# A planner's build-time estimate of the matrix products' pace, replaced by longer steps

## The chip, the core and the metric

The kernel runs on one core of a Trainium2 chip. The metric is the device time of one execution in microseconds (us), lower is better; times of several runs are given as their median.

## The reference

A decoder trunk of two layers in float32, for 256 tokens of 1,024 features, with a memory of 256 rows. Cut to its outline:

```python
for l in range(2):
    h = rms_norm(x, norm_mix[l])
    if l == 0:
        b, c, u = split(h @ conv_w_in, 3)
        x = x + (b * conv3(c * u)) @ conv_w_out
    else:
        x = x + causal_attention(rope(h @ moba_w_q), k, v) @ moba_w_o
    x = x + softmax(q(rms_norm(x)) @ mem_k.T / 16) @ mem_v @ mem_w_o[l]
    g, u = split(rms_norm(x, norm_ffn[l]) @ ffn_w_gu[l], 2)
    x = x + (silu(g) * u) @ ffn_w_down[l]
    if l == 0:
        k, v = split(rms_norm(x, kv_norm) @ w_kv, 2)
        k = rope(k)
return rms_norm(x, norm_final)
```

The feed-forward part has 2,816 hidden features, the memory attention 4 heads of 256, the causal attention 8 heads of 128.

## The kernel before

**Products.** Every large product is made from operands in two float32r parts, a high one and the rest, in three passes: high by low, low by high, high by high. There are two forms. `mm3` (L321) multiplies 128 tokens by up to 512 output features, three products of that width; by `mm_rows` (L419) it serves the projections and `down` (the feed-forward's second half), and with 256 columns the first gate and up products. `mm_cols` (L425) puts output features on partitions: one product of 512 columns (high weights by both parts of 256 tokens) and one of 256 (low weights by the high part), eight such pairs for 128 features; it serves the convolution's gates (tiles `cu`, `pb`), the memory queries (`q_acc`) and most of the gate and up products (`gu`). The keys of the memory (`mem_keys`, L638) use single products of 256 columns. All of them are issued by `mm` (L313, its instruction is L314), transposes by `transpose` (L317, L318).

**Stages.** In order: keys of layer 0's memory (`acc_memk`), the convolution, its output projection (`acc_cout`), the memory's values (`acc_memv`), memory attention, feed-forward (`gu`, `ff`); then layer 1's keys, queries and values (`acc_k`, `acc_q`, `acc_v`), beside the values and the next memory keys the causal attention, its output (`acc_o`), the memory's values, memory attention, feed-forward and the last norm.

**Weights.** They come in chunks of 1,024 columns, 512 KB each, loaded by SyncE (L331) into five raw buffers. ScalarE casts a chunk to its high part, VectorE subtracts to get the low part, and the next raw load follows a low part. Ten chunks may be split ahead of the products (`Feed`, L173).

**Side work.** All that is not this stream (norms, transposes of activations, rotary turns, softmax, the small products of attention) is written as generators. `Side.poll` (L138) is called after each product and lets every generator go on whose time has come; `Feed.pump` then splits a weight chunk if ScalarE or VectorE is free by the estimate and no side step is due within 300 ns. So the place of each instruction in its engine's queue is settled when the program is built, by an estimated clock (`Clock`, L45). The clock keeps for each engine the time at which it is free, and for each written tile the time at which it can be read: an instruction starts when its engine is free and its inputs are ready, and its output is ready 140 ns after its end, 200 ns for TensorE. "Now" is the time at which TensorE is free. `Timed` (L82) estimates ScalarE at 50 + 0.875 ns a column, VectorE at 67 + 1.04, GpSimd at 460, each with 80 more for an operand of one column. A side step that yields nothing goes on at the first poll at which now has reached the readiness of its last instruction; some yield a fixed number of nanoseconds. Where the main stream needs what a side job has not written yet, `Act.need` (L244) lets the job run to its end at once, and TensorE then waits on the chip.

TensorE's costs are given where a product is issued. For a product of n columns:

```python
ns = 0.4167 * math.prod(b[0].shape[1:]) + 2     # mm3
0.4167 * 2 * T + 2,  0.4167 * T + 2             # mm_cols, T = 256
0.4167 * T + 2                                  # mem_keys
```

that is 215.4 ns for 512 columns and 108.7 for 256. Transposes are noted at 109 ns, the causal attention's small products at 218 (436 with 256 columns), and all is doubled while now is under 4,700 ns.

**Side groups named below.** `turned` (L1184): ScalarE copies a bank of keys or queries out of the accumulator (`r`), VectorE turns 32 columns of each head in four steps, TensorE transposes (`pt_r`). `Normed.run` (L761): squares, mean, GpSimd's power (`rs`), the normed rows `hn` on VectorE, transposes (`pt_h`). `attend` in `mem_attention` (L975) and in `moba` (L1213): scores `s`, softmax, transposes of the probabilities (`pt_p`, `pt`), their copy or split `pT`, the product with the values (`po`). `start_rstd` (L615): two diagonals in one buffer, each multiplied by ones (`pb_rs`). `tables` (L791): small loads and, when they should have landed, two small transposes (`pt_c`).

Of the kernel before, what the change touches and what calls it, by code (L numbers as in the profile page):

```python
# [21 lines left out]
KD = D // P  # L22
T = 256
# [10 lines left out]
RAWS = 5  # L34
# [10 lines left out]
class Clock:  # L45
    """Estimates of where the engines stand, in nanoseconds, to choose the order of instructions by."""

# [34 lines left out]
class Timed:  # L82
    """An engine whose instructions are noted on the clock."""

# [23 lines left out]
class Side:  # L108
    """Work beside the main stream of matrix products, as generators. A bare yield waits for the last
    instruction, a number for that many nanoseconds."""  # L110

# [44 lines left out]
    def hold(self, kind):  # L156
        """wait for a free buffer; each is listed with the time from which it is free"""
        free = self.free[kind]
        while not free or min(free) > self.clock.now:
            yield 0 if not free else min(free) - self.clock.now  # L160
        free.remove(min(free))
# [11 lines left out]
class Feed:  # L173
    """The weights in the order of their use: loaded RAWS chunks ahead of their split into two parts,
    which goes on while the engines have nothing else, as far ahead of the products as there are buffers."""

# [58 lines left out]
class Act:  # L235
    """An activation, transposed and in two float32r parts; jobs[half, bank] still fill it."""

# [17 lines left out]
def yoco_kernel(  # L255
# [26 lines left out]

# [1 line left out]
    def acc_tile(name):  # L284
# [26 lines left out]

# [1 line left out]
    def mm(o, l, r, start, stop, ns):  # L313
# [7 lines left out]
    def mm3(o, a, b, start, stop):  # L321
        """a.T @ b of operands in two parts each"""
        ns = 0.4167 * math.prod(b[0].shape[1:]) + 2
        mm(o, a[0], b[1], start, False, ns)
        side.poll()
        mm(o, a[1], b[0], False, False, ns)
        side.poll()
        mm(o, a[0], b[0], False, stop, ns)
# [5 lines left out]

    # ---- weights: a chunk of 1024 columns a partition; a norm's weight goes in here where the
    # chunk's rows are its features ----
    def row_plan(name, w, c0, gain=None, pieces=1, halves=1):
# [42 lines left out]
    def ffn_steps():  # L380
        """pairs of 128 columns: gate and up ahead of down by a pair or more; the last downs come bank by bank"""
        steps, n = [], 0
        for jp in range(NP):
            steps.append(("gu", jp))
            while jp >= ROW_PAIRS and n < min(jp - 2, NP - LAG):
                steps.append(("down", n))
                n += 1
        return steps, list(range(n, NP))
# [28 lines left out]

# [1 line left out]
    def mm_rows(acc, act, k, h, w, b, start, stop):  # L419
        """acc[token, 512 features] += act[token, k-th 128] @ w[k-th 128, 512 features]"""  # L420
        act.need(k, (h,))
        mm3(acc, act.parts(k, tok(h)), [r[:, 0, bank(b)] for r in w], start, stop)
        side.poll()

    def mm_cols(acc, act, w, j):  # L425
        """acc[128 features, (both parts, token)]: its halves' sum is w[:, 128 features].T @ act.T, of the
        chunk's j-th 128"""
        for k in range(KD):
            act.need(k)
            x_both = act.units[k // 4][:, k % 4].rearrange("p r t -> p (r t)")  # L430
            hi, lo = (r[:, k % 4, j * P:(j + 1) * P] for r in w[k // 4])
            mm(acc.rearrange("p r t -> p (r t)"), hi, x_both, k == 0, False, 0.4167 * 2 * T + 2)
            side.poll()
            mm(acc[:, 0, :], lo, act.parts(k)[0], False, k == KD - 1, 0.4167 * T + 2)
            side.poll()
# [15 lines left out]
    def proj_rows(act, name, done, order=STRAIGHT):  # L451
        """act @ w by token halves, k tiles and banks in the order given; done(half, bank, accumulator)"""
        chunks, accs = {}, {}
        for h, k, b in order:
            if (h, b) not in accs:
                accs[h, b] = acc_tile(f"acc_{name}_{h}_{b}")
            if k not in chunks:
                chunks[k] = feed.take(f"{name}_{k}")
            if h == 1 and b == 1:
                feed.free()  # L460
            mm_rows(accs[h, b], act, k, h, chunks[k], b, k == 0, k == KD - 1)
            if k == KD - 1:
                done(h, b, accs[h, b])

    def turn_parts(src, dst, h, g, gain=None):
        """src [128 tokens, 512] to both parts of bank g of dst, features on partitions"""
        yield from side.hold("tp")
        pt = tp_tile("pt_h")
        for i in range(4):
            transpose(pt[:, i, :], src[:, i * P:(i + 1) * P])  # L470
        yield
        if gain is not None:
            yield from side.hold("half")
            t = held_half("xg", (P, 4, P))
            g0 = gain_col(gain, 4 * g)
            g4 = bass.AP(tensor=g0.tensor, offset=g0.offset, ap=[g0.ap[0], [1, 4], [0, P]])
            vector.tensor_mul(t, pt, g4)
            side.give("tp")
            yield
            pt = t  # L480
        yield from split_steps(dst.units[g][:, :, 0, tok(h)], dst.units[g][:, :, 1, tok(h)], pt,
                               "tp" if gain is None else "half")
# [7 lines left out]

# [1 line left out]
    def square_half(src, ss, b):  # L492
# [20 lines left out]

    # ---- constants; the memory, transposed as it is: its norm's weight is in the products' weights and
    # its rows' factors come after the products ----
    ident = const.tile([P, P], F32, name="ident")
# [47 lines left out]
    def warm_up(n):  # L564
        """products that no one reads, for the tensor engine's clock"""
        for _ in range(n):
            transpose(warm[:, :P], ident)
# [68 lines left out]

# [1 line left out]
    def mem_keys(name, mT, wait, ready=None):  # L638
# [16 lines left out]
        def step(k, w, j, passes=((0, 0), (0, 1), (1, 0))):  # L655
            """a bank's two column tiles are one accumulation group: its start clears both"""
            acc = accs[j // 2][:, (j % 2) * T:(j % 2 + 1) * T]
            mT.need(k)
            x = mT.parts(k)
            for a, b in passes:  # L660
                mm(acc, w[a][:, 0, j * P:(j + 1) * P], x[b], k == a == b == 0 and j % 2 == 0,
                   k == KD - 1 and a == 1 and j % 2 == 1, 0.4167 * T + 2)
                side.poll()
# [39 lines left out]

# [1 line left out]
    x_sb = const.tile([P, 2, D], F32, name="x_sb")  # L705
# [12 lines left out]
    class Plain:  # L718
        """x itself, transposed, times a norm's weight if it is not in the products' weights; its rows'
        factors come after the products"""  # L720

# [15 lines left out]
    class Normed:  # L737
        """the normed rows, transposed"""

# [45 lines left out]

# [1 line left out]
    cs = const.tile([P, 2, 2, ROT], F32, name="cs")  # L787
# [82 lines left out]

# [1 line left out]
    def short_conv(act, into):  # L872
# [56 lines left out]

# [1 line left out]
    def softmax(s, p, scale, minus):  # L931
        """scale, minus: the scores' factor and its negative, numbers or a column for each of s's two parts"""
        mx = small.tile([P, 2], F32, tag="mx", name="mx")
# [19 lines left out]

# [1 line left out]
    def mem_attention(l, kT, values, src, into):  # L955
# [77 lines left out]

# [1 line left out]
    def swiglu(l, src, done, fine_end=False, at_end=None):  # L1035
# [21 lines left out]
        def gate_up_rows(jp, w, h):  # L1057
            """one token half, tokens on partitions: it can run before the other half is normed"""
            side.grab("gu")
# [114 lines left out]

# [1 line left out]
    def moba(src, into):  # L1176
# [7 lines left out]
        def turned(dst, key):  # L1184
            """the rows' four heads of a bank, their first 32 columns turned, transposed"""
            def turn(h, b, acc, r):
# [109 lines left out]

# [1 line left out]
    fin = {}  # L1298
# [61 lines left out]
```

## Time and profile before

| | |
|---|---|
| median of three runs | 803.84 us (803.82 to 804.37) |
| span of the profiled execution, first to last instruction | 802.4 us |
| TensorE busy | 792.4 us, 99% |
| VectorE busy | 537.7 us, 67% |
| ScalarE busy | 444.7 us, 55% |
| DMA engines | 54% of 16 engines' span, 143.4 MB |
| granted TensorE clock, mean | 0.996 of 2.4 GHz |

The profiled execution has no time of its own beside its span; the runs' median is 1.4 us longer than that span. PE is TensorE's products, PEld its weight loads (they overlap the products), DVE VectorE, ACT ScalarE, POOL GpSimd, SP SyncE. Matmuls are pipelined and their ends are modelled, so a product is shown for some 390 ns where the next starts after some 227: the pace is read from the starts, or from stretches of many products.

### The profile page before, as it was taken

Reading aid. Unit: us, or ns where it says so; the run is one execution under the profiler, and the core shown is the slowest. Engines: PE = TensorE matmul, PEld = TensorE weight load, DVE = VectorE, ACT = ScalarE, POOL = GpSimd, SP = SyncE. Lnnn points to the kernel's source line nnn. Section 1 sums busy time; section 2 is a strip of 40 time slices with the busy share of each in tenths; the row PEclk is TensorE's granted clock in tenths of the full one; section 3 lists DMA queues with packets and bytes.
Section 4 is the critical chain, followed back from the end, with each engine's and each line's share of the span. In section 5 each row is a group of like instructions: output and inputs, shape, how many; then the busy total and the mean of one; then the engine's idle time right before and its main releaser. Section 6 shows DMA issues by size and latency. Waiting matters only on the chain.

```text
span 802.4 us, 11670 instructions
## 1 busy us (share of the span) xinstructions
PE 792.4 (99%) x4497; PEld 690.8 (86%) x4497; DVE 537.7 (67%) x833; ACT 444.7 (55%) x730; POOL 17.6 (2%) x42
## 2 busy tenths in 40 slices
PE   8999999999999999999999999999999999999996
PEld 7988888898998888888888889888989988888885
DVE  4897987776758655666566667777757576556633
ACT  5766555664656545555554566556645565455432
POOL 0100001000100000000000000010000000000000
PEclk9999999999999999999999999999999999999999
DMA  8666666734547665555466316567344476655611
GB/s 304 222 207 213 214 206 207 244 102 135 155 136 253 197 213 171 160 194 202 136 202 202 139 53 218 176 210 257 112 124 151 138 243 207 210 162 167 199 55 52
DMA packets 90219, 143.40 MB, mean 179 GB/s; under 512 B 4844, under 2 KB 70452, under 8 KB 90164
## 3 DMA queue, kind: packets, MB, share of 16 engines
q1 hardware_dynamic: 89876, 142.14, 54.3%
q8 instruction: 35, 0.57, 0.3%
q10 hardware_dynamic: 288, 0.52, 0.2%
q14 instruction: 20, 0.16, 0.1%
HBM read 141.60 MB, written 1.05 MB: 178 GB/s over the span
## 4 chain that ended last, share of the span: by engine, by line
PE 98%; DMA 1%; SPq 0%; DVE 0%; issue 0%; POOLq 0%; ACT 0%; DVEq 0%; ACTq 0%
PE gu L314 31%; PE ff L314 15%; PE q_acc L314 6%; PE cu L314 6%; PE acc_mo L314 6%; PE acc_memv L314 5%; PE acc_memk L314 5%; PE pb L314 3%; PE acc_v L314 3%; PE acc_q L314 3%; PE acc_cout L314 3%; PE acc_k L314 3%; PE acc_o L314 3%; PE po L314 2%; PE s L314 2%; PE pt_h L318 2%
## 5 line engine op out<-in xcount | busy, mean ns | idle before, releaser
L314 PE MATMUL ff<-hi_wd,guT 128*128 128x512 f32 (+1 forms) x352 | 108.1, 387 | 0.0
L314 PE MATMUL gu<-ffn,hi_wu 128*128 128x512 f32 x288 | 103.2, 398 | 0.0
L314 PE MATMUL gu<-ffn,hi_wg 128*128 128x512 f32 x288 | 103.1, 397 | 0.0
L314 PE MATMUL gu<-ffn,lo_wg 128*128 128x256 f32 x288 | 81.0, 281 | 0.0
L314 PE MATMUL gu<-ffn,lo_wu 128*128 128x256 f32 x288 | 80.8, 281 | 0.0
L314 PEld LDWEIGHTS ff<-hi_wd,guT 128*128 128x128 f32 x352 | 65.7, 188 | 13.4
L103 DVE TENSOR_TENSOR gu_sb<-gu_sb,gu 128x256 f32<-128x256 f32 x72 | 30.3, 421 | 69.6 <-ACT gu_sb L103 69.1
L103 ACT CAST hi_wu<-raw_wu 128x1024 fp32r<-128x1024 f32 x52 | 53.4, 1050 | 35.5 <-PE ff L314 25.0
L103 DVE TENSOR_TENSOR lo_wu<-raw_wu,hi_wu 128x1024 fp32r<-128x1024 f32 x52 | 61.5, 1221 | 14.6 <-ACT hi_wu L103 14.6
L314 PE MATMUL ff<-lo_wd,guT 128*128 128x512 f32 (+1 forms) x176 | 68.4, 388 | 0.0
L103 ACT COPY gu_sb<-gu 128x256 f32<-128x256 f32 x72 | 26.8, 373 | 71.7 <-PE gu L314 71.7
L314 PEld LDWEIGHTS gu<-ffn,hi_wu 128*128 128x128 f32 x288 | 54.1, 188 | 13.4
L314 PEld LDWEIGHTS gu<-ffn,hi_wg 128*128 128x128 f32 x288 | 54.1, 188 | 12.9
L103 DVE TENSOR_TENSOR lo_wd<-raw_wd,hi_wd 128x1024 fp32r<-128x1024 f32 x44 | 53.4, 1221 | 10.1 <-ACT hi_wd L103 10.1
L314 PEld LDWEIGHTS gu<-ffn,lo_wg 128*128 128x128 f32 x288 | 54.4, 189 | 0.5
L314 PEld LDWEIGHTS gu<-ffn,lo_wu 128*128 128x128 f32 x288 | 54.4, 189 | 0.0
L103 DVE TENSOR_TENSOR lo_wg<-raw_wg,hi_wg 128x1024 fp32r<-128x1024 f32 x44 | 52.6, 1219 | 1.1 <-ACT hi_wg L103 1.1
L314 PE MATMUL acc_memk<-mT,hi_memk 128*128 128x256 f32 x256 | 47.8, 291 | 1.8 <-ACT hi_memk L103 1.8
L103 ACT CAST hi_wd<-raw_wd 128x1024 fp32r<-128x1024 f32 x44 | 45.8, 1046 | 4.2 <-PE ff L314 4.2
L103 ACT CAST hi_wg<-raw_wg 128x1024 fp32r<-128x1024 f32 x44 | 45.6, 1051 | 0.6 <-PE acc_mo L314 0.6
L314 PE MATMUL q_acc<-mem,hi_mq 128*128 128x512 f32 x128 | 45.9, 399 | 0.0
L314 PEld LDWEIGHTS acc_memk<-mT,hi_memk 128*128 128x128 f32 x256 | 40.0, 195 | 2.1 <-ACT hi_memk L103 2.0
(229 smaller groups left out, 1823.7 us busy)
## 6 DMA issues: line engine op xcount, KB each, us to landing
raw_wg<-in_ffn_w_gu_dram SPq DMA_DIRECT2D x44, 512.0 KB, 4.8
raw_wu<-in_ffn_w_gu_dram SPq DMA_DIRECT2D x44, 512.0 KB, 3.7
raw_wd<-in_ffn_w_down_dram SPq DMA_DIRECT2D x44, 512.0 KB, 4.3
raw_memv<-in_mem_w_kv_dram SPq DMA_DIRECT2D x16, 512.0 KB, 4.6
raw_mq<-in_mem_w_q_dram SPq DMA_DIRECT2D x16, 512.0 KB, 5.0
raw_mo<-in_mem_w_o_dram SPq DMA_DIRECT2D x16, 512.0 KB, 4.7
raw_memk<-in_mem_w_kv_dram SPq DMA_DIRECT2D x14, 512.0 KB, 5.4
raw_wc<-in_conv_w_in_dram SPq DMA_DIRECT2D x8, 512.0 KB, 3.7
```

Of the source, the lines that this page charges most:

```text
L103: return call(out, *args, **kw)
L314: nc.tensor.matmul(o, l, r, start=start, stop=stop)
L318: nc.tensor.transpose(o, i, ident[:i.shape[0], :i.shape[0]])
```

## The change

A function gives the cost of a product of n columns on the estimated clock, and the three forms use it. No instruction is added or removed by the diff itself. What else the diff holds are comments and texts of functions that are dropped. The core:

```diff
+    def mm_ns(n):
+        return n / 2.4 + 13.5
...
     def mm3(o, a, b, start, stop):
-        ns = 0.4167 * math.prod(b[0].shape[1:]) + 2
+        ns = mm_ns(math.prod(b[0].shape[1:]))
...
     def mm_cols(acc, act, w, j):
...
-            mm(acc.rearrange("p r t -> p (r t)"), hi, x_both, k == 0, False, 0.4167 * 2 * T + 2)
+            mm(acc.rearrange("p r t -> p (r t)"), hi, x_both, k == 0, False, mm_ns(2 * T) + 8)
             side.poll()
-            mm(acc[:, 0, :], lo, act.parts(k)[0], False, k == KD - 1, 0.4167 * T + 2)
+            mm(acc[:, 0, :], lo, act.parts(k)[0], False, k == KD - 1, mm_ns(T) - 3)
             side.poll()
...
         def step(k, w, j, passes=((0, 0), (0, 1), (1, 0))):
...
                 mm(acc, w[a][:, 0, j * P:(j + 1) * P], x[b], k == a == b == 0 and j % 2 == 0,
-                   k == KD - 1 and a == 1 and j % 2 == 1, 0.4167 * T + 2)
+                   k == KD - 1 and a == 1 and j % 2 == 1, mm_ns(T))
                 side.poll()
```

The estimates become 226.8 ns for 512 columns and 120.2 for 256, and 234.8 and 117.2 for the pair in `mm_cols`.

## Rows read from the trace of the kernel before

**Rows 1.** The page, parts 1 and 4: busy engines; the chain's shares.

```profile
PE 792.4 (99%) x4497; PEld 690.8 (86%) x4497; DVE 537.7 (67%) x833; ACT 444.7 (55%) x730; POOL 17.6 (2%) x42
...
PE 98%; DMA 1%; SPq 0%; DVE 0%; issue 0%; POOLq 0%; ACT 0%; DVEq 0%; ACTq 0%
```

**Rows 2.** TensorE's waits: us in total, times, longest us.

```profile
PE acc_memk L314 <- ACT hi_memk L103: 1.8, 1, 1.8
```

**Rows 3.** The chain in order of time: start us, us, what, how many.

```profile
46.27 5.55 PE cu L314 x32
...
104.51 11.38 PE acc_cout L314 x50
...
261.33 11.29 PE gu L314 x64
...
488.07 16.67 PE acc_memk L314 x139
```

**Rows 4.** Timeline, a turned pair of layer 1's keys: start us, us, what [idle before].

```profile
407.46 1.31 ACT L103 ACTIVATE r<-acc_k,rs 128x512 f32<-128x512 f32 x2 [5.67 <-PE acc_k L314]
...
408.71 0.36 DVE L103 TENSOR_TENSOR r<-rope 128x64 f32<-128x64 f32 x2
...
409.19 0.42 PEld L318 LDWEIGHTS pt_r<-ident,r 128*128 128x128 f32 x4 [0.21 <-issue]
409.24 0.60 PE L318 MATMUL pt_r<-ident,r 128*128 128x128 f32 x4
...
409.70 0.36 DVE L103 TENSOR_TENSOR r<-rope 128x64 f32<-128x64 f32 x2
```

**Rows 5.** Busy time of acc_k's instructions in that stretch: us, then PE, PEld, ACT.

```profile
407.19:409.20 2.01, 2.01 (x10) 1.50 (x8) 1.31 (x2) 1.00 0.02 8
```

**Rows 6.** Chain, then timeline: layer 0's second token half normed for the feed-forward.

```profile
208.89 6.94 PE gu L314 x58
...
212.35 1.46 POOL L103 TENSOR_TENSOR rs<-ms,neg_half 128x1 f32<-128x1 f32 x1 [10.22 <-DVE ms L103]
...
213.85 1.41 DVE L103 SCALAR_TENSOR_TENSOR hn<-x_sb,rs,g_ffn 128x512 f32<-128x512 f32 x2 [0.44 <-POOL rs L103]
...
215.67 0.60 PE L318 MATMUL pt_h<-ident,hn 128*128 128x128 f32 x4
```

**Rows 7.** Timeline, probabilities by values: the causal attention's, then the memory attention's.

```profile
477.09 0.59 ACT L103 COPY pT<-pt 128x512 f32<-128x512 f32 x1 [0.82 <-PE pt L318]
...
477.78 1.10 PE L314 MATMUL po<-pT,v_sb 128*128 128x128 f32 x8
...
193.01 0.69 DVE L103 TENSOR_TENSOR pT<-pt_p,pT 128x512 fp32r<-128x512 f32 x1 [2.03 <-ACT pT L103]
...
193.99 1.59 PE L314 MATMUL po<-pT,memv 128*128 128x256 f32 x12
```

**Rows 8.** Timeline, two places where weight loads stood: the first keys, the output projection.

```profile
30.02 0.29 DVE L103 TENSOR_SCALAR diag<-ident,m_rs 128x128 f32<-128x128 f32 x1 [1.19 <-PE pb_rs L314]
...
31.55 0.19 PEld L314 LDWEIGHTS acc_memk<-mT,lo_memk 128*128 128x128 f32 x1 [0.33 <-DVE lo_memk L103]
...
196.23 0.69 DVE L103 TENSOR_TENSOR oT_mem<-po,oT_mem 128x512 fp32r<-128x512 f32 x1
...
196.98 0.30 PEld L314 LDWEIGHTS acc_mo<-hi_mo,oT_mem 128*128 128x128 f32 x2 [0.46 <-DVE oT_mem L103]
```

**Rows 9.** The chain again: the convolution's start, and first gates in both layers.

```profile
37.48 2.36 PE cu L314 x13
39.83 0.23 PE pt_c L318 x2
40.06 3.44 PE cu L314 x19
...
234.92 20.93 PE gu L314 x121
...
635.07 21.32 PE gu L314 x121
```

## The prediction, made before the change was built

> **What bounds the kernel now.** I read the page first. TensorE is busy for 792.4 us, 99% of the span, and the chain of work that ended last is 98% TensorE [rows 1]. The list of its waits names almost nothing behind the first 12 us; it has three entries, and the longest, 1.8 us, is for the first weights [rows 2]. So the kernel's time is the length of one stream of 4,497 products plus some 12 us of start and 6 us of end, and side work costs only where that stream has to stand still for it. Faster side work is worth nothing else.
>
> Next I read the chain of waits for the stream's real pace [rows 3]. 50 products of 512 columns take 11.38 us, 227.6 ns each; 139 of 256 columns 16.67 us, 119.9 ns each; a 512 and a 256 together 352.8 ns in the feed-forward part (11.29 us for 32 pairs) and 346.9 ns in the convolution (5.55 us for 16). The old estimates for the three are 215.4, 108.7 and 324.0 ns; the new ones 226.8, 120.2 and 352.0. The new ones are right to within 1.5%, the old ones were 5, 10 and 8% too fast. The Trainium skill, "TensorE: Matmul & The Clock Gate" (Back-to-back issue gap), gives N / 2.4 + 2.5 ns for a warm product, 215.7 ns at 512 columns, which is the old estimate almost to the digit and speaks against this change; by it the new clock would be the one that runs wrong, and each group moved ahead would meet products of 215.7 ns, which adds about 0.09 us to each stall of 8 steps worked out below, some 0.7 us over the eight turned groups. The 50 products of [rows 3] decide against it here, and the sums below go by 227 ns.
>
> **What the change does.** It removes and adds no instruction. The planner polls after each product and lets a side step go when the estimated clock has passed the time at which its input is ready. Product estimates grow by 11.5 ns, or 28 ns a pair; the costs of ScalarE, VectorE, GpSimd and loads, the 140 and 200 ns of latency and the timers stay. So each side step, and each weight split and load that a split triggers, is written 5 to 10% earlier, counted in products. For ScalarE and VectorE that changes only the order in their queues: they still start when their inputs are there. For SP it changes which load is issued at which product; the loads wait for a split's low part on VectorE anyway, and the stream ran into no weight that was still on its way behind 12 us [rows 2]. The splits up to ten chunks ahead are the cover, so I price this at 0; without it a late chunk's wait would stand in TensorE's list. For transposes and small products, which stand in TensorE's own stream, it takes away slack: TensorE gets there earlier while the data chain behind them keeps its length. Everything in the stream queues behind such a wait.
>
> **The slack that goes.** For each kind of side group I compare the moment its last input was written with the moment TensorE started on it.
>
> *Turned rows (pt_r, 8 groups).* Planned latency after the product: 200, then 578 + 140 on ScalarE, 2 x 200 + 2 x 134 + 140 on VectorE, 1,725 ns. That is 8.01 old steps, so 9 products were put before the transposes; [rows 5] counts ten in that window, one of them still running at its start. It is 7.61 new steps, so there will be 8. On the chip the last VectorE write ends at 409.07, the weight load follows at 409.19 after idling 0.21 us, the transposes at 409.24 [rows 4]: the stream was just not held up. One product of 227 ns fewer in front means a stall of about 0.2 us, since the data come no sooner (ScalarE was idle for 5.67 us before this chain [rows 4]). The second group of the pair, whose rows are written until 410.06 [rows 4], loses a product too. 8 x 0.19 = **1.5 us**. Bounds 0, if the eighth product hides it, and 8 x 0.23 = 1.8.
>
> *Normed rows for the feed-forward part (pt_h from hn, one tight group a layer).* Between the attention's last product and this group stand 58 products of 256 columns [rows 6], 6.30 us of the old clock; 53 fill that time on the new one, 0.6 us less in the real stream. The real margin is 215.67 - 215.26 = 0.41 us [rows 6], and some 0.15 of it is needed, the distance that [rows 4] shows from 409.07 to 409.24. The plan is too short mainly by GpSimd's power, planned at 460 ns and 1.46 us long [rows 6]. So 0.6 - 0.26 = 0.33 us a layer, **0.65 us**. Bounds 0 and 1.2.
>
> *Products of probabilities and values (po).* In layer 1's causal part the plan is 200 + 498 + 140 = 838 ns, 7.7 old steps of 256 columns (8 products) and 6.97 new ones (7). The margin is 477.78 - 477.68 = 0.1 us [rows 7], already nothing; three such groups run in this stream, so 3 x 0.12 = **0.35 us**. In the memory attention the plan is 1,577 ns, 7.3 old steps of 512 columns and 6.95 new, one product fewer; the margin is 193.99 - 193.70 = 0.29 us [rows 7], so 0.06 us for each of four: **0.25 us**. Bounds for both together 0 and 3 x 0.12 + 4 x 0.23 = 1.3.
>
> The transposes of the residual stream (plan 940 ns: 4.4 and 4.1 steps, 5 products both times) do not move and cost nothing.
>
> Sum of new stalls: 1.5 + 0.65 + 0.35 + 0.25 = **+2.75 us**, between 0 and 4.3. I take values near the upper ends because the margins read from [rows 4, 6, 7], less the 0.1 to 0.15 us that a start needs, are all smaller than what is lost. Below 0 is excluded for these terms: a group that comes earlier makes the stream no shorter by itself.
>
> **What is gained.** Places where the stream waits for side work that came too late. At 31.55 a weight load had idled 0.33 us for a low part, because VectorE had stood 1.19 us before a diagonal until the product of the diagonal before it was done [rows 8]; that product comes earlier now: -0.3 us. In both layers the output projection of the memory attention reaches its last head before that is written (VectorE until 196.92; the weight load at 196.98 had idled 0.46 us [rows 8], though products before it still ran): I take -0.15 each. Sum **-0.6 us**. No gain beyond that, since nothing else in the stream waits.
>
> Net +2.15 us on the profiled execution, whose span is 802.4 us. The runs' median of 803.84 lies 1.4 us above the span, and I take that surrounding as unchanged: **806.0 us**.
>
> **The rivals.**
>
> *The pace locks otherwise.* The trace shows two steady paces of the 512 + 256 pair. The convolution starts at the slow one (13 products in 2.36 us), two small transposes interrupt it at 39.83, and behind them it runs at the quick one (19 in 3.44 us, then 32 in 5.55) to its end, 186 pairs later [rows 3, 9]. The first gate and up products run quick in layer 0 and slow in layer 1, the same 121 products in 20.93 and 21.32 us [rows 9]. An interruption seems to choose. (a) Against the kernel: those transposes hang on loads and timers of the estimated clock, and 192 products of the memory's keys come before, which the new clock makes 2.2 us longer. They were 2.4 us into the convolution, so they land about at its start; if before it, the convolution may keep the slow pace, 186 x 5.9 ns = 1.1 us more: 807.1 us with the stalls. (b) On the other side, faster: an interruption in the queries' 128 slow pairs (0.75 us) and in layer 1's first gates (0.39 us) lets them run quick; with the 0.6 us gained and none of the stalls, 803.84 - 1.75 = 802.1 us. It decides from the first pair behind a transpose in those two stages. Against it: the queries have been interrupted by scores and transposes in both layers already and stayed slow.
>
> *The margins hold.* Side steps written earlier also move ahead of weight splits in the queues of ScalarE and VectorE, so the data chains get shorter where they stood behind a split, and the groups arrive in time. For it: VectorE is busy for 67% and ScalarE for 55% of the span [rows 1], so a chain often meets a split. Against: the turned groups' chain had an idle ScalarE before it [rows 4]. Then only the gains count: 803.2 us, with half of the stalls 804.6.
>
> *Nothing moves.* Most groups keep their product because polls are discrete, as those of the residual stream do: 803.8 us.
>
> **How the numbers follow.** Forecast, stalls without a changed pace: 0.42, own range 805.0 to 807.0. Stalls and a slow convolution: 0.18. Margins hold: 0.24. Nothing moves: 0.08. Paces turn quick: 0.08. A measurement of this kernel can tell about 0.2%, 1.6 us, from no change, so faster means under 802.2 and slower over 805.4. Slower holds three quarters of the first case and nearly all of the second, 0.50; faster holds the last and a tail of the third, 0.09; the rest, 0.41, is no change. The range runs from 802.9 (margins hold, with 0.3 us of a quicker pace) to 807.6 (stalls at their upper bounds, 803.84 + 4.3 - 0.6, or with a slow convolution), which leaves out the quick paces and the far tail above.
>
> **What would show it.** Right: each pt_r group one product earlier, its weight load idle some 0.2 us longer, its start still 0.17 us behind VectorE's last write; the load at 31.55 and the stop at 196.98 gone; the sum of TensorE's rows unchanged and the stretch 398 to 444 us of the kernel about 1.5 us longer. Wrong: 32 products of the convolution in 5.64 us instead of 5.55 would put part of the time on the pace; a new wait for a DMA or a split in the list of TensorE's waits would mean that feeding, which I priced at nothing, decides. If the eight pt_r groups come one product earlier and no weight load idles longer, the chains were shorter than I think, and the forecast falls to the case in which the margins hold.

## The result, and the profile after

The changed kernel takes **809.76 us** (median of six runs, 808.71 to 813.12) against 804.36 (803.82 to 806.05) for the kernel before on the same chip: ratio **1.0087** [1.0071, 1.0103]. It is slower, as forecast, but by 5.4 us instead of 2.15, and outside the range. The profiled execution took 811.91 us, 2.15 above that median, its span 809.8. The page, parts 1 and 4, as in [rows 1]:

```profile
PE 795.0 (98%) x4497; PEld 691.2 (85%) x4497; DVE 539.0 (67%) x833; ACT 444.0 (55%) x730; POOL 15.6 (2%) x42
...
PE 89%; DVE 4%; DMA 3%; ACT 2%; issue 1%; POOL 0%; SPq 0%; POOLq 0%; ACTq 0%; DVEq 0%
```

The same instructions, the same busy times within 3 us, but the chain that ended last is 89% TensorE where it was 98%: work of other engines stands on the path now. The list of TensorE's waits (columns as in [rows 2]):

```profile
PE acc_memk L318 <- ACT hi_memk L103: 2.9, 1, 2.9
PE pt_h L322 <- DVE ffn L103: 1.4, 2, 0.7
...
PE cu L318 <- DVE conv L103: 0.9, 2, 0.7
PE acc_mo L318 <- DVE oT_mem L103: 0.9, 1, 0.9
PE pt_h L322 <- DVE hn L103: 0.4, 2, 0.2
PE acc_mo L318 <- ACT oT_mem L103: 0.3, 1, 0.3
```

Five new entries, at three places (the convolution, the memory attention's output, the first gates), and the turned rows, the forecast's largest term, are not among them. (Lines after L312 stand four further down than before.)

To see where the time went, take from both timelines the start of the first product of each stage and subtract. Behind the start, from the first `cu` on, the profiled executions differ by 6.46 us, more than the medians do:

| stretch, first product to first product | before, us | after, over before |
|---|---|---|
| convolution (`cu` to `acc_cout`) | 67.04 | +1.90 |
| layer 0, memory output (`acc_mo` to `gu`) | 28.35 | +1.48 |
| layer 0, first gates (`gu` to the 97th `gu`) | 12.58 | +1.35 |
| keys and queries (`acc_k` to `acc_v`) | 47.32 | +0.63 |
| layer 1, memory output | 28.29 | -0.14 |
| layer 1, first gates (`gu` to the 193rd of the layer) | 24.52 | +1.35 |
| all the rest behind the first `cu` | 556.96 | -0.12 |

The start itself is 0.97 us longer, which can't be put down to the change: two programs that are the same up to there (this one and `hold_later` below) reached the first `cu` at 38.28 and 34.45 us, and three others that are the same (`late_conv`, `conv_and_later`, `conv_later_turn`) at 34.48, 36.17 and 36.88. So stages behind it are compared, and the runs' medians for the whole.

**What happened at the three large places.** ScalarE takes its list in order (the rows below show it), and at each of them a weight cast now stands in that list ahead of a side step and waits.

*Convolution.* ScalarE's timeline (start us, us, what [idle before]), after, then before:

```profile
75.15 1.06 ACT L103 CAST hi_wc<-raw_wc 128x1024 fp32r<-128x1024 f32 x1 [0.89 <-DMA raw_wc<-in_conv_w_in_dram]
...
77.84 1.05 ACT L103 CAST hi_wu<-raw_wu 128x1024 fp32r<-128x1024 f32 x1 [0.97 <-DMA raw_wu<-in_conv_w_in_dram]
80.16 1.05 ACT L103 CAST hi_wu<-raw_wu 128x1024 fp32r<-128x1024 f32 x1 [1.27 <-DMA raw_wu<-in_conv_w_in_dram]
81.12 0.36 ACT L103 COPY conv<-cu 128x256 f32<-128x256 f32 x1
...
81.99 0.50 PE L318 MATMUL cu<-mix,hi_wc 128*128 128x512 f32 x1 [0.70 <-DVE conv L103]
```

```profile
79.23 1.05 ACT L103 CAST hi_wu<-raw_wu 128x1024 fp32r<-128x1024 f32 x1 [3.01 <-DMA raw_wu<-in_conv_w_in_dram]
80.18 0.36 ACT L103 COPY conv<-cu 128x256 f32<-128x256 f32 x1
80.70 1.05 ACT L103 CAST hi_wu<-raw_wu 128x1024 fp32r<-128x1024 f32 x1 [0.16 <-DMA raw_wu<-in_conv_w_in_dram]
```

The sum that is copied at 81.12 was complete when the next tile's products began, at 75.46; the copy stood behind two casts of chunks that were still being loaded. Its buffer is wanted again two `cu` tiles later, at 81.29 (81.99 less the 0.70 waited), so TensorE stood. Before, too, a copy stood behind a cast that waited 3.01 us for its chunk, but behind one, and the buffer came free in time.

Not all of the 1.90 us is standing still. A first, smaller wait for the same reason (at 66.89) and this one, with the products right behind them, come to some 1.6 us from start to start. Between the two, 16 products take 2.82 to 2.83 us where they took 2.77 before, the slower of the two paces of [rows 9]; behind the second the stretch runs at 2.77 again. Some 40 pairs at 5.9 ns more are about 0.25 us, an estimate from these rows.

*Layer 0's memory output.* After:

```profile
198.42 1.05 ACT L103 CAST hi_wu<-raw_wu 128x1024 fp32r<-128x1024 f32 x1 [2.98 <-PE acc_mo L318]
199.38 0.57 ACT L103 CAST oT_mem<-po 128x512 fp32r<-128x512 f32 x1
199.50 1.23 DVE L103 TENSOR_TENSOR lo_wu<-raw_wu,hi_wu 128x1024 fp32r<-128x1024 f32 x1 [3.34 <-ACT hi_wu L103]
...
200.01 0.50 PE L318 MATMUL acc_mo<-lo_mo,oT_mem 128*128 128x512 f32 x1 [0.26 <-ACT oT_mem L103]
200.65 0.68 DVE L103 TENSOR_TENSOR oT_mem<-po,oT_mem 128x512 fp32r<-128x512 f32 x1
...
201.39 0.73 PE L318 MATMUL acc_mo<-hi_mo,oT_mem 128*128 128x512 f32 x2 [0.88 <-DVE oT_mem L103]
```

The cast waits 2.98 us for a weight buffer that products still read. Before, the same cast stood ahead of the same step, but the products that free the buffer came ahead of the last head's `po` (cast at 193.96, `po` at 193.99 [rows 7]); now `po` comes first (196.22) and the freeing products behind it, while `oT_mem`, made from `po`, stands behind the cast. VectorE repeats it: the late chunk's low part (199.50) stands ahead of the low part of `oT_mem` (200.65), for which TensorE waits a second time, 0.88 us. In layer 1 the order came out with `oT_mem` first, and the stretch is 0.14 us shorter than before.

*First gates, both layers alike.* ScalarE, VectorE and TensorE in layer 0, after, then before:

```profile
211.31 0.60 PE L322 MATMUL pt_h<-ident,hn 128*128 128x128 f32 x4
211.51 1.05 ACT L103 CAST hi_wu<-raw_wu 128x1024 fp32r<-128x1024 f32 x1 [1.68 <-PE acc_mo L318]
212.46 0.63 ACT L103 ACTIVATE junk<-x_sb 128x512 bf16<-128x512 f32 x1
...
213.09 0.57 ACT L103 CAST ffn<-pt_h 128x512 fp32r<-128x512 f32 x1
...
213.69 0.69 DVE L103 TENSOR_TENSOR ffn<-pt_h,ffn 128x512 fp32r<-128x512 f32 x1 [1.04 <-ACT ffn L103]
214.29 0.68 DVE L103 TENSOR_TENSOR x_sb<-x_sb,acc_mo 128x512 f32<-128x512 f32 x1
...
220.10 0.63 PE L322 MATMUL pt_h<-ident,hn 128*128 128x128 f32 x4 [0.20 <-DVE hn L103]
...
222.13 0.65 PE L322 MATMUL pt_h<-ident,hn 128*128 128x128 f32 x4 [0.69 <-DVE ffn L103]
```

```profile
207.07 0.59 ACT L103 CAST ffn<-pt_h 128x512 fp32r<-128x512 f32 x1 [1.65 <-PE pt_h L318]
...
208.15 0.68 DVE L103 TENSOR_TENSOR ffn<-pt_h,ffn 128x512 fp32r<-128x512 f32 x1
208.18 1.04 ACT L103 CAST hi_wu<-raw_wu 128x1024 fp32r<-128x1024 f32 x1
...
208.93 0.69 DVE L103 TENSOR_TENSOR x_sb<-x_sb,acc_mo 128x512 f32<-128x512 f32 x1
```

Before, `ffn` is cast as soon as its transposes end. After, a cast waiting for a buffer and a square come first; VectorE's subtraction waits 1.04 us for `ffn`, and the last addition to the residual stands behind that in VectorE's list. It comes 1.16 us after the first `gu` product (213.13) instead of 0.20 (208.73). From it runs the chain of mean, power and `hn` [rows 6], and its transposes stop TensorE twice.

The Trainium skill, "Perfetto Trace Analysis" (Sequencer Loop), says that an engine's instructions are read one after another and wait for their semaphores; the trace agrees at each place: the step behind the cast begins right after it (81.12, 199.38, with no idle time of their own).

### The profile page after: what moved, and what is told of

Its sections match the earlier page's. It is cut to its first block, busy times and chain, and to the rows that moved or that the text cites. A ratio compares the mean times of both kernels' runs of the same rounds, so it can differ in the third digit from the quotient of the medians.

```text
span 809.8 us, 11695 instructions
## 1 busy us (share of the span) xinstructions
PE 795.0 (98%) x4497; PEld 691.2 (85%) x4497; DVE 539.0 (67%) x833; ACT 444.0 (55%) x730; POOL 15.6 (2%) x42
## 4 chain that ended last, share of the span: by engine, by line
PE 89%; DVE 4%; DMA 3%; ACT 2%; issue 1%; POOL 0%; SPq 0%; POOLq 0%; ACTq 0%; DVEq 0%
PE gu L318 29%; PE ff L318 15%; PE q_acc L318 6%; PE acc_memk L318 5%; PE acc_memv L318 5%; PE acc_mo L318 5%; PE acc_v L318 3%; PE acc_q L318 3%; PE acc_o L318 3%; PE acc_cout L318 3%; PE acc_k L318 3%; PE po L318 2%; PE cu L318 2%; PE s L318 2%; DMA raw_wu<-in_conv_w_in_dram 2%; PE pt_h L322 2%
```

## The experiments

**Theories.** *Casts in the way*, as above. *Lost slack*, the prediction's: transposes and small products come earlier than their data. And later a third: *any other order costs*, because the other constants of the planner fit the old estimate.

### Which user of the estimate, and which form

Two kernels keep a second clock with the old estimate beside the new one: in `side_new` the side steps go by the new one and the weight splits by the old one, in `feed_new` the other way round.

```diff
+    clock.twin = Clock()
...
-        clock.note("pe", ns, [o], [l, r], 200)
+        clock.note("pe", ns, [o], [l, r], 200, old_ns(ns))
...
-    feed = side.feed = Feed(clock, plan, load_chunk, split_high, split_low)
+    feed = side.feed = Feed(clock.twin, plan, load_chunk, split_high, split_low)
```

> Two estimated clocks are kept: side steps go by the new pace, weight splits and their loads by the old one. Theory 1 (side groups lost their slack, so TensorE meets data that is not there yet): the waits of TensorE for turned rows (0.6 us in all in the changed kernel) and for the normed rows of the feed-forward (1.3 us a layer) stay, and the time is 3 to 4 us over the kernel before, about 807.5 us. Theory 2 (splits written earlier stand in ScalarE's queue before side steps, waiting for a load or a buffer): those waits go with the splits, the convolution takes the 67.0 us of the kernel before, and the time is under 805.5 us.

> The other way round: side steps by the old pace, weight splits by the new one. Theory 1: nothing is lost, 804 us. Theory 2: the convolution keeps the stalls of the changed kernel (1.9 us there, from a cast that waits for its load ahead of the copies that free an accumulator), and the time is 2 to 4 us over the kernel before. Both theories together: about 806.5 us, with no wait for turned or normed rows.

Measured: `side_new` 814.29 us, ratio 1.0118 [1.0103, 1.0133]; `feed_new` 815.29, 1.0123 [1.0101, 1.0144]. Over the kernel before, convolution +4.27 and +5.99, first gates +0.47 and +1.44 in each layer, keys and queries +0.69 and +0.05. So the gates' loss goes with the splits, and the turned rows' with the side steps, as each theory says of its part. But both theories' times were missed, for each half alone is slower than the whole: two clocks that disagree bring stalls of their own (1.2 us at a product of `acc_cout` in `side_new`, 3.1 at a product of `cu` in `feed_new`), and these two can't be added. In `feed_new`, TensorE's granted clock behind that wait of 3.1 us was 0.50 of 2.4 GHz, its lower level, from 43.6 to 48.6 us, so the stall cost more than itself.

The other split is by form: `rows_only` has the new estimate in `mm3` alone, `cols_only` in `mm_cols` alone.

> The new estimate in the three-pass products alone (projections, first gates, down), the old one in the column pairs and the memory's keys. Theory 1: the turned rows and the normed rows lie in this form's streams, so their waits stay (0.6 us and twice 1.3 us), about 807 us, and the convolution, whose order on ScalarE is that of the kernel before, takes 67.0 us. If the clock's whole drift since the start decides, rather than the pace within a chain, the loss is only in part there.

> The new estimate in the column pairs alone (convolution, memory queries, most gates). Theory 2: both casts of a pair of chunks stand ahead of the accumulator's copy on ScalarE here too, so the convolution is 1 to 3 us longer than 67.0 us; no wait for turned or normed rows; about 806 us. If the stall in the convolution came from the memory's keys before it (an earlier start of all side work), it is gone here: 804 us.

Measured: 808.3 us, 1.0048 [1.0031, 1.0064], and 806.89, 1.0024 [1.0014, 1.0034]. `rows_only`: convolution 0.00, gates +1.36 and +1.35, keys and queries +1.01. `cols_only`: convolution +2.24, gates 0.00 and -0.01, keys and queries +0.09. The convolution's and the gates' losses sit where the changed form is in use, so these are local. Layer 0's output lost in neither (-0.19 and -0.05), so the order that costs 1.48 us there came about only with both.

### The planner more careful everywhere

Four kernels on top of the changed one: `hold_1000` splits no chunk while a side step falls due within 1,000 ns instead of 300; `late_loads` plans every chunk's landing 2,500 ns later; `lag_150` puts 150 ns on each side step; `hold_late_lag` has all three.

```diff
-HOLD = 300
+HOLD = 1000
...
-        clock.note("dma", 1.43 * math.prod(dst.shape[1:]), [dst], [], 900)
+        clock.note("dma", 1.43 * math.prod(dst.shape[1:]), [dst], [], 900 + late)
...
-            item[0] = self.clock.last if pause is None else self.clock.now + pause
+            item[0] = self.clock.last + 150 if pause is None else self.clock.now + pause
```

> The changed kernel, but no weight chunk is split when a side step is due within 1,000 ns instead of 300. On ScalarE the cast of the chunk that stood ahead of the second norm's squares (layer 0 and 1) now stands behind them, and the last head's output ahead of its cast. Theory 2 (a cast that waits for a buffer or a load, ahead of side steps): the first gates take the time of the kernel before in both layers (1.3 us less each than in the changed kernel), the output projection of layer 0 loses its 1.5 us, and the time is about 4 us under the changed kernel's, 805 to 806.5 us; the turned rows' waits stay. Theory 1 (side groups without slack): the waits of the normed rows stay, 809 us or more.

> The changed kernel, but the estimate lets a weight chunk land 2,500 ns later, so that its cast is written later. Theory 2: the convolution loses most of its 1.9 us, the other stalls stay: 807 to 808.5 us. Theory 1: nothing changes, 809.8 us.

> The changed kernel, but each side step waits 150 ns longer behind its input on the estimated clock, about the slack that the old pace gave. Theory 1: no turned row makes TensorE wait (0.6 us), and the normed rows lose most of their 1.3 us a layer; 806.5 us. Theory 2: the turned rows' 0.6 us go, but the normed rows, the convolution and the output projection keep theirs: about 809 us.

> The three together on the changed kernel: hold of 1,000 ns, loads 2,500 ns later, steps 150 ns later. If the two theories name all that was lost, each wait is gone and the time is that of the kernel before or a little less, 803 to 804.5 us. If moving the order by itself costs, whatever the direction, it stays over 806 us.

Measured, us and ratio to the kernel before on that chip (802.76): 813.16, 1.0126 [1.0111, 1.0141]; 814.57, 1.0145 [1.013, 1.016]; 812.22, 1.0122 [1.0102, 1.0143]; 806.08, 1.004 [1.0026, 1.0054]. At the aimed place each did its work: with `hold_1000` gates at +0.16 and +0.14 and layer 0's output at -0.23; with `late_loads` convolution at +0.90, with no wait left in it (16 products take 2.82 to 2.83 us from its second tile to its end, the slower pace); with `lag_150` keys and queries at +0.29. Elsewhere they lost again: `hold_1000` and `lag_150` +6.35 and +6.02 in the convolution, and `late_loads` reached its first `cu` at 39.90 us, the latest of all. `hold_late_lag` was to take 803 to 804.5 us and missed that; its 806.08 lies at the bound of 806 above which any move of the order was to be what costs. Behind the first `cu` it lost only 1.11 us (convolution +1.43, gates +0.71 and +0.22, keys and queries +0.06); where the rest of its 3.3 us lies isn't shown, as the kernel before has no trace on that chip. A setting for the whole program can't test a local cause.

### One place at a time

`hold_later` is `hold_1000` from the first memory attention on; `late_conv` is `late_loads` for the convolution's chunks alone.

```diff
+    side.near = 1000
     mem_attention(0, memk0, memv0, in_mem0, in_ffn0)
...
-            load(raw[:, :, i * n:(i + 1) * n], src[:, :, i * n:(i + 1) * n])
+            load(raw[:, :, i * n:(i + 1) * n], src[:, :, i * n:(i + 1) * n],
+                 2500 if it['name'][:2] in ('wc', 'wu', 'wb') else 0)
```

> The changed kernel, with the planner's HOLD of 300 ns (no weight chunk is split while a side step falls due within it) raised to 1000 ns from the first memory attention on; start, keys and convolution are written as in the changed kernel. Casts in the way (ScalarE takes its instructions in order, and a weight cast written ahead of a side step and waiting for its buffer holds that step up): the first gates of each layer fall from 1.4 us over the kernel before to 0.2 or less, layer 0's memory output projection from 1.5 to 0.3 or less, the convolution stays at 1.9 over, the turned rows' stall stays (0.3 to 0.7); whole kernel 3.0 to 4.5 us over the kernel before (ratio 1.0037 to 1.0056). Lost slack alone (the data is not there in time, whatever stands ahead): the gates' 1.4 us stay, and the whole stays at about 5.4 us (1.0067). Any disturbance costs: the gates improve, but the later parts lose as much again (in the run with 1000 everywhere the second layer's later gates lost 1.5), total 5 us or more.

> The changed kernel, with the landing time that the planner takes for the convolution's weight chunks 2500 ns later, and for no others. Casts in the way: the casts of the convolution's chunks are no longer written ahead of the copies of its sums while their loads are still under way, and the convolution (first product of cu to first of acc_cout) falls from 1.9 us over the kernel before to 1.0 or less, with nothing lost at the start, as no other chunk's time is touched; gates (1.4 each) and turned rows stay; whole kernel 3.8 to 5.0 over (1.0047 to 1.0062). Lost slack: the convolution stays at 1.9 or more, whole 5.4 or more. Any disturbance costs: the convolution moves its stalls elsewhere and loses 2 us or more.

Measured: 806.82 us, 1.0059 [1.0038, 1.0081], and 807.38, 1.0055 [1.0033, 1.0077] (kernel before 802.7). `late_conv`: convolution -0.01, all else as in the changed kernel (+1.44 output, +1.34 and +1.33 gates, +0.67 keys and queries). ScalarE's timeline there:

```profile
69.82 1.05 ACT L103 CAST hi_wu<-raw_wu 128x1024 fp32r<-128x1024 f32 x1
71.26 0.38 ACT L103 COPY conv<-cu 128x256 f32<-128x256 f32 x1 [0.38 <-PE cu L318]
71.53 0.41 ACT L103 CAST yT<-conv 128x256 fp32r<-128x256 f32 x1
71.94 1.05 ACT L103 CAST hi_wu<-raw_wu 128x1024 fp32r<-128x1024 f32 x1
74.03 0.38 ACT L103 COPY conv<-cu 128x256 f32<-128x256 f32 x1 [1.04 <-PE cu L318]
```

Copies wait for their products and for nothing else, casts for nothing: the whole 1.90 us is gone, more than the expected half. `hold_later`: output -0.23, gates +0.52 (over the 0.2 expected; 0.4 of it at the transposes of `gg`, another tile) and +0.14. The convolution missed: +3.06, though written as in the changed kernel. Its start came 3.8 us sooner, and at 36.66 the two small transposes `pt_c` waited for their load, 0.53 us. The two waits for casts with the products right behind them came to 1.8 us, near the 1.6 of the changed kernel. The rest is the pace, which stayed slow from the first of them (63.9) to the end of the convolution. From the chain, behind the second wait, in `hold_later` and then in the changed kernel:

```profile
87.75 5.65 PE cu L319 x32
```

```profile
90.74 5.55 PE cu L318 x32
```

In the feed-forward parts it also lost 0.57 and 0.71 us, with one wait for `gu_sb` in each, and layer 0's later gates ran at the slower pace (+0.38). ScalarE and VectorE at the first gates:

```profile
206.60 0.59 ACT L103 CAST ffn<-pt_h 128x512 fp32r<-128x512 f32 x1 [1.48 <-PE pt_h L323]
...
207.44 0.68 DVE L103 TENSOR_TENSOR ffn<-pt_h,ffn 128x512 fp32r<-128x512 f32 x1
...
209.18 0.68 DVE L103 TENSOR_TENSOR x_sb<-x_sb,acc_mo 128x512 f32<-128x512 f32 x1
209.19 1.99 ACT L103 CAST hi_wu<-raw_wu 128x1024 fp32r<-128x1024 f32 x2
```

The casts stand behind the side step again, and the last addition comes 0.47 us after the first `gu` (208.71) instead of 1.16.

### Half the step, and a step the other way

Every estimate halfway between old and new (`step_half`), and as much shorter than the old one as the change makes it longer (`step_back`, so further from the trace); the pair's own terms, 8 and -3, are scaled alike:

```diff
-        return n / 2.4 + 13.5
+        return n / 2.4 + 2 + 5.75
...
-        return n / 2.4 + 13.5
+        return n / 2.4 + 2 + -11.5
...
```

> Half of the change: every estimate halfway between the old and the new one (5.75 ns more a product instead of 11.5). If the cost comes with how much too long the planner takes a product for (slack given away step by step), it is about half of the change's: 1.5 to 3.5 us over the kernel before (1.002 to 1.0045), with the turned rows at 0.1 to 0.4 and the gates at 0.4 to 1.0 each. If the old estimate is only the one at which the other constants were set, and any other order brings chance stalls, it is 4 us or more (1.005 up), with the gates at 1.4 (its cast hi_wu stands between the two ffn casts as in the full change) and the layer 0 projection at 0 to 1.5. Casts in the way says, from the order written: gates 1.2 to 1.5 in each layer, layer 0's output projection 0 to 1.5.

> The change the other way: every estimate as much shorter than the old one as the change makes it longer (11.5 ns less a product), so further from the steps of the trace. Slack given away: side steps are written later against the products than before, so no data is late that was not late before; turned rows 0, hn of the first gates 0; the whole kernel within 1 us of the kernel before (0.9988 to 1.0012). Casts in the way: depends on the order alone; here hi_wu stands between the two ffn casts as in the changed kernel, so the first gates lose 1 us or more in each layer, and the convolution's casts stand one by one as in the kernel before, so it loses under 1 us; whole 2 to 4 us (1.0025 to 1.005). Constants set for the old estimate: 4 us or more (1.005 up).

Measured: `step_half` 807.9 us, 1.0068 [1.0046, 1.009]; `step_back` **810.14**, 1.009 [1.0066, 1.0113]. Half the step costs about three quarters of the whole one, and the step away from the trace costs as much as the step towards it. TensorE's waits in `step_back`:

```profile
PE gu L318 <- DVE ffn L103: 1.9, 2, 1.0
...
PE acc_mo L318 <- DVE oT_mem L103: 1.1, 2, 0.9
...
PE acc_mo L318 <- ACT oT_mem L103: 0.3, 1, 0.3
```

Output +1.43 and +0.85, gates +1.57 twice; keys and queries are 0.28 shorter, and no turned row waits. The convolution's +1.23 is no stall: no product waits there, and 32 products of `cu` take 5.65 us from 44.57 us on, as in `hold_later` behind its waits. The small transposes `pt_c` interrupted it at 37.8 us, and the pace stayed slow. The whole, 7.4 us over the kernel before, is outside the 2 to 4 that casts in the way gave. In `step_half` gates +1.22 twice, the output -0.34 in layer 0 but +1.45 in layer 1, keys and queries +0.07. In both, the `hi_wu` cast stands between the two `ffn` casts as in the changed kernel, but the last link is another one. VectorE and TensorE in `step_back`:

```profile
210.36 1.22 DVE L103 TENSOR_TENSOR lo_wu<-raw_wu,hi_wu 128x1024 fp32r<-128x1024 f32 x1
...
211.50 0.68 DVE L103 TENSOR_TENSOR ffn<-pt_h,ffn 128x512 fp32r<-128x512 f32 x1
...
212.24 0.50 PE L318 MATMUL gu<-hi_wg,ffn 128*128 128x256 f32 x2 [0.97 <-DVE ffn L103]
```

Here a low part stands ahead of a side step on VectorE, busy and not waiting, and the first product that needs that step stands: again a split in the way. So lost slack isn't the main cause: with slack given back, `step_back` loses as much. Of four estimates the old one, wrong by 5 to 10%, gives the best order.

### All places together

`conv_and_later` joins `late_conv` and `hold_later`; `conv_later_turn` also plans the turning of rows to end 500 ns later.

```diff
                 vector.tensor_add(v[:, :, HR:ROT], t[:, 0, :, HR:], t[:, 1, :, :HR])
+                clock.last += 500
                 yield
```

> The changed kernel with both edits together: the convolution's chunks taken 2500 ns later by the planner, and HOLD 1000 ns from the first memory attention on. If casts in the way are the cause, the two gains add, since they lie in different stages: convolution 0 over the kernel before, layer 0's output projection under 0.1, first gates 0.6 or less in each layer, later gates 0.6 and turned rows 0.5 together left; whole kernel 1.7 to 3.0 us over the kernel before (ratio 1.002 to 1.0037), that is at most half of the change's loss. If any disturbance costs about the same whatever its place, it stays at 4 us or more (1.005 up).

> As the one above, and the planner takes the turning of the keys' and queries' rows to end 500 ns later, so that their transposes are written later in the stream. Lost slack (the rows' data was not there when their transposes came up): the transposes wait for nothing and the keys' and queries' products (first of acc_k to first of acc_v) fall to within 0.1 us of the kernel before, from 0.4 to 0.6 over; whole kernel 0.4 us less than the one above (1.2 to 2.6 over the kernel before, 1.0015 to 1.0032). If the wait has another cause (the buffers of tp, or ScalarE's list), the keys and queries stay at 0.4 over or more.

Measured, 12 runs each: 805.46 us, 1.0019 [1.0008, 1.003], 1.2 us over the kernel before where 1.7 to 3.0 were expected, and **804.3, 1.0005 [0.9992, 1.0017]** (kernel before 804.23). The changed estimate with three local edits of the planner costs nothing that can be measured. In `conv_later_turn` the list of TensorE's waits has two entries, both before the first `cu`. Its second turned group of the keys (weight load and transposes):

```profile
410.18 0.60 PEld L323 LDWEIGHTS pt_r<-ident,r 128*128 128x128 f32 x4
410.42 0.60 PE L323 MATMUL pt_r<-ident,r 128*128 128x128 f32 x4
```

In the changed kernel that group looks so:

```profile
415.57 0.36 DVE L103 TENSOR_TENSOR r<-rope 128x64 f32<-128x64 f32 x2
...
416.04 0.42 PEld L322 LDWEIGHTS pt_r<-ident,r 128*128 128x128 f32 x4 [0.41 <-issue]
416.07 0.63 PE L322 MATMUL pt_r<-ident,r 128*128 128x128 f32 x4
```

There the weight load follows 0.11 us behind VectorE's last write (415.93, the end of 415.57 plus 0.36) after idling 0.41; with 500 ns in the plan it idles for nothing. So the turned rows did wait for their own data. Keys and queries went from +0.50 in `conv_and_later` to -0.48, but the stretch behind them to `acc_mo` from +0.23 to +0.65, so some of that only moved. In both, layer 0's later gates ran at the slower pace (+0.39). Neither kernel beats the one before.

## Why the prediction was right and wrong

**What bounds, right.** Side work costs only where TensorE's stream stands for it; the chain's fall from 98 to 89% is just that. The pace of single products did not change (50 products of `acc_cout` in 11.37 us, as in [rows 3]); the 215.7 ns that follow from the formula of the Trainium skill, "TensorE: Matmul & The Clock Gate" (Back-to-back issue gap), do not show here either. That section gives the formula for an isolated product, so the prediction read it too widely.

**The step that failed.** "For ScalarE and VectorE that changes only the order in their queues: they still start when their inputs are there", and the splits priced at 0 because ten chunks ahead "are the cover". The cover is for the products, and no product waited for a weight behind the start. But a split whose chunk has not landed, or whose buffer is still read, waits at the head of ScalarE's list, and a side step written behind it waits too. That one sentence holds the convolution (1.90, with the slower pace that lay between its waits), layer 0's output (1.48) and most of the first gates (1.35 twice). [Rows 8] and ScalarE's timeline of the convolution showed it could: there a cast waited 3.01 us with a copy behind it. The forecast said a wait for a split in the list of TensorE's waits would prove this step wrong; it was one link further off, a wait for what stands behind a split.

**Term by term.** *Turned rows*: mechanism right, size wrong. All eight groups were to come one product earlier and lose 0.19 us each. Only two came earlier, the second group of the first pair of the keys and of the queries (1 product of the stream between it and the group before, where 2 stood); both stalled, some 0.3 us each, and the stretch is 0.63 us longer, not 1.5. The other six stand behind as many products as before (54 before the first group of the keys, both times; weight load idle 0.21 us, as in [rows 4]), so the count of 9 and 8 in the prediction is wrong for them. *Normed rows*: forecast 0.33 a layer, measured 1.35. TensorE's wait for `hn` itself is 0.2 each; the 0.7 for `ffn` behind it comes from the late addition, and `hold_later` took most of both away. *Products of probabilities and values*: forecast 0.6, measured 0.27 at most by stretches (`acc_v` to `acc_o` +0.18, `acc_cout` to `acc_mo` +0.05, `acc_o` to layer 1's `acc_mo` +0.04). *Gains*: the 0.15 for the last head came in layer 1 (-0.14) and turned into the loss of 1.48 in layer 0. The 0.3 at the first keys can't be read through the start's own spread.

**The rivals.** The pace did turn, twice. The 121 products of layer 1's gates took 20.93 us instead of 21.32 [rows 9], the -0.35 in the last part of the table's rest; and the convolution ran slow between its two waits, about 0.25 us. So "the pace locks otherwise" holds a small part of the result, though not as forecast: it was the waits, not the transposes `pt_c`, behind which the pace turned, and with the casts out of the way the convolution took 67.03 us against 67.04. The slow convolution that the prediction priced at 1.1 us did come in `step_back` (+1.23) and `late_loads` (+0.90). "Margins hold" rested on side steps moving ahead of weight splits; at the costly places splits moved ahead of side steps, since both go by the same clock and a split is written whenever no side step is due within 300 ns.

**What stays open.** Why the old estimate gives a good order was not tried further, nor what decides which pace a stretch of pairs takes: it changed behind a wait in some places and stayed in others. That three of three other values lose at the gates and at one memory output or both, and that edits of three other constants win it all back, fits constants chosen at the old value; it does not prove it.

## What to carry to other kernels

A planner's estimate is one of a set of constants: making one of them truer, alone, reorders the lists, and here the true pace cost as much as one wrong the other way. When work moves within an in-order list, ask of each entry not only what it costs but what it can wait for, and who stands behind it; a wait of an engine that is busy for 55% can still set the end. Test such a cause by an edit at its place, not by a setting for the whole program.

## What was not expected of the hardware

Two programs with the same instructions up to the first convolution product reached it 3.8 us apart (38.28 and 34.45 us).

A wait can cost more than its own length. Behind a wait of 0.24 us at 66.89 the changed kernel's convolution went on at the slower pace until the next wait; in `hold_later`, behind one of 0.11 us at 63.47, it kept that pace to its end. And behind a wait of 3.1 us in `feed_new` the granted clock was 0.50 for the 5 us from 43.6 on, then 1.00 (each row: the stretch; its us; busy us of TensorE's products, its weight loads, VectorE, ScalarE and GpSimd; granted clock; DMA share; GB/s):

```profile
43.60:48.60 5.00, 5.00 (x15) 4.24 (x16) 4.00 (x7) 2.52 (x4) 0.00 (x0) 0.50 0.98 318
49.00:54.00 5.00, 5.00 (x31) 4.38 (x30) 3.81 (x6) 2.62 (x5) 0.00 (x0) 1.00 0.39 133
```
